# Negated gates at the end of a later pool, DRAM weight sums in 2 KB packets at other places, and the loaded sum first in its tile

## The chip, the cores and the metric

The kernel runs on one core of a Trainium2 chip. The metric is the device time of one execution in microseconds (us); the profile is of one execution, whose span begins with its first instruction. Engines are named as in the profile: PE (matrix unit; PEld is its weight load), DVE, ACT, POOL, and SP, which here only issues DMAs. The granted clock is the share of PE's full clock that the throttle let through.

## The reference, cut to what matters

Two layers over 512 latent tokens and 256 context tokens, width 1024, all float32. Layer 0 mixes tokens by windowed attention with a sink, layer 1 by retention in both directions; after each stands a SwiGLU feed-forward network (FFN). Both are modulated by a shift, scale and gate (adaLN).

```python
def modulate(h, shift, scale):
    return h * (1 + scale) + shift

def swiglu(h, w_in, w_out):
    gate, up = jnp.split(h @ w_in, 2, axis=-1)
    return (jax.nn.silu(gate) * up) @ w_out
```

The kernel needs float32 accuracy from a matrix unit that is given operands in a shorter form. Each float32 tile is therefore split into a high part (a cast on ACT) and a low part (the difference, on DVE), and each product is three matmuls: high by high, low by high, high by low.

## The kernel before, in words

**Order.** The code is written in the order of the data. A planner then orders the instructions of each engine by estimates of when operands are ready and results due; `after(ins, others)` (L97) adds an order that the planner has to keep, with no wait of its own. Each engine runs its own list strictly in order. A tile name with a number of buffers rotates through them: a new tile waits until the old content has been read.

**Attention (about 100 to 322 us).** `attend` (L800) does one block of queries for one group of four heads; the loop at L909 makes 24 such turns, 0 to 23, six for each of four groups. Between them `make_q` (L583) makes the queries of two heads: after turns 1, 3, 7, 9 and 13 for the pairs j = 3 to 7, and once ahead of the loop for j = 2. For j from 2 to 6 the high half is cast into a tile `y0` with one buffer, the low half into `hn`, and four DMAs for each token stream bring the halves to their partitions (L626, issued by SP). Tiles `k1`, `k2` of the keys come from `key_parts` (L568). At turns late in the loop the residual streams are loaded (L180, L187) and the weights of the output projection Wo (L128), both on SP.

**The FFN of layer 0 (about 421 to 776 us).** The FFN is written as a seven-product scheme on 2 x 2 blocks, so it needs sums of weight blocks. For positions 2 to 21 two of the sums are made ahead in DRAM: `gu_sum`, five positions in each of four batches, and for the output weights `fo_sum` in two batches. `sum_copy` (L828) copies a weight block to DRAM on SP's queue; `sum_add` (L831) adds another with a DMA that accumulates, on POOL's queue. Each batch of `gu_sum` takes two copies and two adds (1280 KB each), each batch of `fo_sum` four copies and four adds, of which two copies start from the sum made before. `spread` hangs these steps on turns: a step is issued behind the last copy of that turn's block. Turns from 100 on are positions of the FFN. Each step on SP or POOL that depends on an earlier one waits there, and what is behind it in that queue waits too.

`seven(pos)` (L1123) does one position: it loads two weight tiles `g` and `u` and the sum `t1` (L1127 to L1130), splits g into b11, t1 into w1 (`bhi`, `blo`), forms two more weight sums on DVE (L1136, L1137), splits them into b24 (`whi`, `wlo`), splits u into b3, and runs seven products at L970: in the order that PE gets, Y from b11, X from b11, Z from w1, Y from b24 and so on. The c11 add (L1150) brings Y and X together on DVE ahead of the first silu. In most positions one step of the next layer's adaLN vectors (L276, L279) is done as well.

**Output products (776 to about 985 us).** `fo_product` (L1197) runs pairs of positions; for each it loads the tokens (`fo_tokens`) and weights (`fo_weights`, L1185), splits them and multiplies at L1207. Its argument `ahead` says behind which pair's first product other work may go. `fo_add` (L1212) adds the result to the residual stream, with a gate or, where the scheme subtracts, with the negated gate `ngate`.

**Pools.** SBUF is shared out by pools that lie one behind the other: those of one side from the bottom, those of the other side (`side="right"`) from the top. `cp`, in which `ngate` lies (64 bytes in each partition), is the first on the left; the pools opened after it on that side, `ap`, `ep`, `fp` and so on, stand above it. `T(pool, cols, name, bufs)` takes a tile from a pool.

Of the kernel before, what the change touches and what calls it, by code (L numbers as in the profile page):

```python
# [8 lines left out]
F32 = mybir.dt.float32  # L9
# [5 lines left out]
P = 128  # L15
# [8 lines left out]
FT = DFF // P  # L24
FFN_GROUPS = (2, 4, 4, 4, 4, 4)
PAIRS = FT // 2
TURN = [p + PAIRS * j for p in range(PAIRS) for j in range(2)]
GU_BATCH, GU_BATCHES = 5, 4
ROW = 8192
FO_BATCHES = (6, 5)  # L30
RH = 4
EPS = 1e-6
# [22 lines left out]
def dit_kernel(ctx, tc, xT, cT, crow, small, consts, masks, tabs0, tabs1, jtab, adaQ, adaN, adaT, wst, wgu, wfo, out):  # L55
    nc = tc.nc
    mult, add, sub = ALU.mult, ALU.add, ALU.subtract
# [9 lines left out]
    def T(pool, cols, tag, bufs, dt=F32):  # L67
        return pool.tile([P, cols], dt, tag=tag, bufs=bufs, name=tag)

    def pj(n=512):  # L70
# [10 lines left out]
    mods = {(l, s): cp.tile([P, 6, 8], F32, name=f"mod{l}{s}") for l in range(2) for s in range(2)}  # L81
    acol = {(l, s, w): cp.tile([P, 8], F32, name=f"acol{l}{s}{w}")
            for l, s, w in ((0, 0, 0), (0, 1, 0), (0, 0, 1), (0, 1, 1), (1, 0, 0), (1, 1, 0), (1, 0, 1))}
    ngate = cp.tile([P, 2, 8], F32, name="ngate")
    gm2 = cp.tile([P, 32], F32, name="gm2")
    nc.vector.tensor_scalar(gm2, sm_t[:, C_G:C_G + 32], -2.0, None, op0=mult)
    qk_gain = cp.tile([P, 2], F32, name="qk_gain")
# [9 lines left out]
    def after(ins, others):  # L97
        for o in others:
            tc.add_manual_dep(ins.ins, o.ins.name, order, reason="table set turn")
# [69 lines left out]
    def split(t, hi, lo, behind=()):  # L169
        after(nc.scalar.copy(hi, t), behind)  # L170
        return nc.vector.tensor_tensor(lo, t, hi, op=sub)  # L171
# [389 lines left out]
    At = ExitStack()  # L561
    ap = At.enter_context(tc.tile_pool(name="ap", bufs=1, reuse_waits="tile"))

    kx, kc = {}, {}
    off_grid(ap, 16)

    def key_parts(e, src, tag="k", bufs=8):
        if tag == "kc":  # L568
            both = T(akv, 1024, tag, bufs, F32R)
            k1, k2 = both[:, 0:512], both[:, 512:1024]  # L570
        else:
            k1, k2 = T(akv, 512, tag, bufs, F32R), T(akv, 512, tag, bufs, F32R)
        src = src[64 * e:64 * e + 64, :]
        nc.scalar.copy(k1[0:64, :], src)
        nc.scalar.copy(k2[64:128, :], src)
        hi_same = (k1[0:64, :], k2[64:128, :])[e]
        nc.vector.tensor_tensor(k1[64:128, :], src, hi_same, op=sub)
        nc.vector.tensor_tensor(k2[0:64, :], src, hi_same, op=sub)
        return k1, k2

    q, stats, norm_end = {}, {}, []
# [81 lines left out]
    with tc.manual_schedule(engines={mybir.EngineType.PE}):  # L663
        q0[0]()
        key_factor(1)
        for e in range(2):
            kx[e] = key_parts(e, kn[0])
        q0[1]()
        c1()
        for e in range(2):  # L670
            k1, k2 = key_parts(e, kn[1], "kc", 2)
            kc[e], kc[2 + e] = ((k1[:, c], k2[:, c]) for c in HALVES)
        q0[2]()
        values(0, 3)
        q0[3]()
        values(1, 2)
        values(1, 3)
# [147 lines left out]
    fo_sum = [dp.tile([4, n, P, 512], F32, name=f"fo_sum{b}") for b, n in enumerate(FO_BATCHES)]  # L825

    def sum_copy(dst, src, behind):
        after(nc.sync.dma_start(flat(dst), flat(src)), [behind])  # L828

    def sum_add(dst, src, behind):  # L830
        after(nc.gpsimd.dma_start(flat(dst), flat(src), accum_op=add, max_dma_last_dim=ROW), [behind])  # L831
# [1 line left out]
    def gu_steps(b):  # L833
        rows = slice(2 + b * GU_BATCH, 2 + (b + 1) * GU_BATCH)
        t = gu_sum[b]
        return [lambda a: sum_copy(t[0], wgu[0, rows], a), lambda a: sum_copy(t[1], wgu[2, rows], a),
                lambda a: sum_add(t[0], wgu[2, rows], a), lambda a: sum_add(t[1], wgu[3, rows], a)]

    def fo_steps(b):
        rows = slice(sum(FO_BATCHES[:b]), sum(FO_BATCHES[:b + 1]))  # L840
        t = fo_sum[b]
        return [lambda a: sum_copy(t[3], wfo[0, rows], a), lambda a: sum_copy(t[2], wfo[2, rows], a),
                lambda a: sum_add(t[3], wfo[2, rows], a), lambda a: sum_add(t[2], wfo[3, rows], a),
                lambda a: sum_copy(t[0], t[3], a), lambda a: sum_add(t[0], wfo[3, rows], a),
                lambda a: sum_copy(t[1], t[0], a), lambda a: sum_add(t[1], wfo[1, rows], a)]

    sum_turns = {}

    def spread(steps, turns):
        for st, n in zip(steps, turns):  # L850
            sum_turns.setdefault(n, []).append(st)

    spread(gu_steps(0), (1, 2, 4, 5))
    spread(gu_steps(1), (5, 6, 8, 9))
    spread(gu_steps(2), (9, 10, 12, 13))
    spread(gu_steps(3), (13, 14, 16, 17))
    spread(fo_steps(0), (3, 7, 11, 15, 17, 19, 21, 23))
    spread(fo_steps(1), range(102, 118, 2))

    for piece in make_q(1):  # L860
        piece()
    rope_key(kn[2])
# [30 lines left out]
    early = [2, 3, 0, 1]  # L893
# [224 lines left out]
    def ada_next(behind):  # L1118

        if ada_q:  # L1120
            ada_tile(*ada_q.pop(0), cr, [behind], fp)

    def seven(pos):  # L1123
        g, u = raw_turn(), raw_turn()
        t1 = op_t()[:, 0:512]
        sums = gu_sum[(pos - 2) // GU_BATCH][:, (pos - 2) % GU_BATCH]
        nc.sync.dma_start(two(g), rows_of(wgu[0:2, pos]))  # L1127
        nc.sync.dma_start(t1, sums[0])
        nc.sync.dma_start(u[:, 512:1024], wgu[3, pos])
        nc.sync.dma_start(u[:, 0:512], sums[1])  # L1130
        l_, r_ = slice(0, 512), slice(512, 1024)
        b11 = w_parts(fp, 1)
        split(g, *b11)
        w1 = T(fp, 512, "bhi", 1, F32R), T(fp, 512, "blo", 1, F32R)
        split(t1, *w1)
        nc.vector.tensor_tensor(g[:, l_], t1, u[:, r_], op=add)  # L1136
        nc.vector.tensor_tensor(g[:, r_], g[:, r_], g[:, l_], op=add)  # L1137
        b24 = w_parts(fp, 1)
        half = split(g, *b24)
        b3 = w_parts(fp, 1)  # L1140
        split(u, *b3)
        if cr:
            ada_next(half)
        X, Y, Z = bank("X"), bank("Y"), bank("Z")
        c11, c12, c22, c21 = t_hn(384), t_hn(384), t_sq(384), t_sq(384)
        a = new_act(pos % 2)
        product(Y, operand["11"], b11, 0, True)
        nc.scalar.copy(c11, Y)
        product(X, operand["12"], b11, 512, True)
        nc.vector.tensor_tensor(c11, c11, X, op=add)  # L1150
        silu(c11, c11)
        product(Y, operand[2], b24, 0, False)
        nc.scalar.copy(c12, Y)
        product(Z, operand[1], w1, 0, True)
        nc.scalar.copy(c21, Z)
        product(Y, operand[3], b3, 0, False)
        nc.scalar.copy(c22, Y)
        nc.vector.tensor_tensor(c22, c21, c22, op=sub)
        product(Z, operand[4], b3, 512, False)
        nc.vector.tensor_tensor(c12, Z, c12, op=sub)  # L1160
        finish_half(a, 0, c11, c12)
        product(Y, operand["22"], b24, 512, False)
        silu(c21, Y)
        end = finish_half(a, 1, c21, c22)
        return pair_sums() if pos % 2 else end
# [24 lines left out]
    def fo_tokens(i, m, n):  # L1190
        raw = op_t()
        load = nc.sync.dma_start(raw[:, 0:384 * n].rearrange("p (a n) -> p a n", a=n), rows_of(saved[m][i, 0:n]))
        x = T(ep, WIDE, "aq", 8, F32R), T(ep, WIDE, "aq", 8, F32R)
        split(raw[:, 0:384 * n], *(t[:, 0:384 * n] for t in x))
        return x, load

    def fo_product(o, i, kind, first, per_step=(), ahead={}):  # L1197
        for m in range((PAIRS + 1) // 2):
            n = min(2, PAIRS - 2 * m)
            x, load = fo_tokens(i, m, n)  # L1200
            w = fo_weights(kind, m, n, load)
            for j in range(n):
                xs = [t[:, j * 384:(j + 1) * 384] for t in x]
                for d in range(4):
                    ws = slice(j * 512 + d * P, j * 512 + (d + 1) * P)
                    for e, (p, r) in enumerate(((w[0], xs[0]), (w[1], xs[0]), (w[0], xs[1]))):
                        ins = nc.tensor.matmul(o[d], p[:, ws], r, start=first and 2 * m + j + e == 0,  # L1207
                                               stop=2 * m + j == PAIRS - 1 and e == 2, skip_group_check=True)
                        if j + d + e == 0 and m in ahead:
                            late, n_late = ahead[m]  # L1210
                            after(ins, late[:n_late])
            for go in per_step[m:m + 1]:  # L1212
                go(ins)
# [56 lines left out]
    for pos in range(2, FT):  # L1270
        if pos == 2:
            last_sum()
        end = seven(pos)
        if pos == 2:
            ends.pop(0)()
            for s in range(2):
                nc.vector.tensor_scalar(ngate[:, s], mods[0, s][:, 5], -1.0, None, op0=mult)
        if pos == 4:
            cr = cond_rows(fp)
        for st in sum_turns.get(100 + pos, ()):  # L1280
            st(end)
        if pos > 3 and pos % 6 != 5:
            ada_next(end)
# [60 lines left out]

    early, ctx_sum = [], []
    y = [bank("Y"), bank("Y"), bank("Z"), bank("Z")]
    fo_product(y, 3, 5, True, [first_half, first_half_norm], {3: (early, 1), 4: (early, 2)})
    fo_add(y, 0, 1)
    F.close()
    E.close()  # L1350
# [775 lines left out]
```

## Time and profile before

| | |
|---|---|
| median of 3 runs (range) | 1815.34 us (1812.19 to 1816.35) |
| profiled execution | 1814.74 us |
| its span | 1813.0 us |
| mean granted clock of PE | 0.985 |
| PE busy | 1730.4 us (95%) |
| DVE, ACT, POOL busy | 1336.5, 890.4, 112.3 us |
| DMA | 98216 packets, 297.83 MB, mean 164 GB/s |

The page gives busy time of each engine over the span, the granted clock and the DMA share by slices, the queues, the chain of work that ended last, and the costliest groups of instructions. The views of the trace that the prediction uses are: waits (an engine and line, what it waited for, total us, times, longest), stretches (busy time of each engine between two times, with clock and DMA share), DMA issues (line of the program, size, median time to landing) and instructions in order of time (start, length, engine, line, out<-in).

### The profile page before, as it was taken

What the parts mean: (1) busy time and instruction counts of PE and PEld (TensorE: products, weight loads), DVE (VectorE), ACT (ScalarE), POOL (GpSimd) and SP (SyncE); (2) the same over time, 40 slices, a digit from 0 to 9 for tenths busy, and PEclk for the clock granted to TensorE, in tenths of its full rate; (3) what the DMA queues carried; (4) which work ended last, traced back from release to release, by engine and by line L of the source; (5) the groups of instructions that cost most, each with busy time, mean ns of one, the idle gap of its engine ahead of it and who ended that gap; (6) DMA issues with size and microseconds to landing.
All of it is one profiled execution on the core that took longest, in us unless ns stands there. A gap on an engine that the chain in (4) does not pass through costs nothing.

```text
span 1813.0 us, 27982 instructions
## 1 busy us (share of the span) xinstructions
PE 1730.4 (95%) x10798; PEld 1548.3 (85%) x10798; DVE 1336.5 (74%) x2385; ACT 890.4 (49%) x1555; POOL 112.3 (6%) x246
## 2 busy tenths in 40 slices
PE   8999989998888988989998999999999999999999
PEld 5877767898888888889997889889888899999998
DVE  6787668796676676777778876776757898777874
ACT  5586668464333333344455453534534564445442
POOL 0001111000111111110000000000000010000000
PEclk9999899999999999999999999999999999999999
DMA  9538788644476657589735471453533333333332
GB/s 374 191 106 233 204 210 227 221 140 166 154 214 212 198 186 209 180 317 306 264 115 143 106 208 48 129 163 77 169 105 95 103 106 104 94 116 96 104 92 82
DMA packets 98216, 297.83 MB, mean 164 GB/s; under 512 B 10161, under 2 KB 22209, under 8 KB 94625
## 3 DMA queue, kind: packets, MB, share of 16 engines
q1 hardware_dynamic: 80656, 222.69, 36.8%
q0 software_dynamic: 17136, 72.82, 16.5%
q8 instruction: 85, 1.39, 0.3%
q10 hardware_dynamic: 288, 0.52, 0.1%
q14 instruction: 51, 0.41, 0.1%
HBM read 274.82 MB, written 61.28 MB: 185 GB/s over the span
## 4 chain that ended last, share of the span: by engine, by line
PE 48%; DVE 3%; DMA 3%; issue 1%; ACT 1%; DVEq 0%; ACTq 0%
PE Z L1443 7%; PE Y L970 6%; PE Y L1432 3%; PE Z L970 3%; PE pj L1443 2%; PE pj L153 2%; PE pj L155 2%; PE pj L154 2%; PE X L1432 2%; PE X L970 1%; DMA adaw<-in_adaT_dram 1%; PE X L1443 1%; PE Y L1207 1%; PE Z L1207 1%; PE Y L154 1%
## 5 line engine op out<-in xcount | busy, mean ns | idle before, releaser
L171 DVE TENSOR_TENSOR wlo<-wraw,whi 128x1024 fp32r<-128x1024 f32 (+1 forms) x285 | 343.5, 1209 | 95.7 <-ACT whi L170 94.9
L170 ACT CAST whi<-wraw 128x1024 fp32r<-128x1024 f32 (+1 forms) x285 | 293.8, 1038 | 234.6 <-DMA wraw<-in_wst_dram 46.2
L970 PE MATMUL Y<-aq,whi 128*128 128x384 f32 x640 | 181.1, 346 | 2.1 <-ACT whi L170 2.1
L970 PEld LDWEIGHTS Y<-aq,whi 128*128 128x128 f32 x640 | 119.7, 192 | 8.6 <-ACT whi L170 4.3
L970 PE MATMUL Y<-aq,wlo 128*128 128x384 f32 x320 | 109.5, 342 | 2.8 <-DVE wlo L171 2.8
L279 DVE CUSTOM_DVE_ANT_0 y<-adaw,crow,small_sb 128x1024 bf16<-128x1024 f32 x64 | 82.0, 1282 | 39.2 <-DMA adaw<-in_adaT_dram 38.8
L1443 PE MATMUL Z<-whi,sA 128*128 128x512 f32 x256 | 81.3, 394 | 0.0
L107 ACT ACTIVATE pr<-pr,stat,qs 128x513 f32<-128x513 f32 (+2 forms) x96 | 74.2, 774 | 9.6 <-DVE stat L735 8.1
L170 ACT CAST aq<-op 128x768 fp32r<-128x768 f32 (+1 forms) x62 | 41.8, 692 | 57.6 <-PE pj L1207 27.8
L155 PE MATMUL pj<-ax,whi 128*128 128x512 f32 x176 | 68.9, 392 | 0.0
L153 PE MATMUL pj<-ax,whi 128*128 128x512 f32 x176 | 68.8, 391 | 0.0
L154 PE MATMUL pj<-ax,wlo 128*128 128x512 f32 x176 | 68.8, 391 | 0.0
L970 PEld LDWEIGHTS Y<-aq,wlo 128*128 128x128 f32 x320 | 61.4, 192 | 4.7 <-DVE wlo L171 4.4
L754 PE MATMUL pT<-const_sb,pr 128*128 128x128 f32 x352 | 56.2, 283 | 9.6 <-ACT pr L743 4.8
L970 PE MATMUL Z<-aq,bhi 128*128 128x384 f32 x160 | 49.5, 373 | 13.6 <-ACT bhi L170 13.6
L970 PE MATMUL Y<-sA,whi 128*128 128x256 f32 x304 | 59.8, 281 | 0.0
L262 DVE SCALAR_TENSOR_TENSOR res<-pj,mod,res 128x512 f32<-128x512 f32 (+1 forms) x64 | 45.4, 714 | 18.9 <-PE pj L155 18.7
L729 DVE CUSTOM_DVE_ANT_0 pr<-S,mask,qs 128x256 f32<-128x256 f32 (+1 forms) x96 | 53.4, 569 | 7.2 <-PE S L728 5.3
L970 PE MATMUL Y<-hx,whi 128*128 128x256 f32 x304 | 57.8, 281 | 0.0
L754 PEld LDWEIGHTS pT<-const_sb,pr 128*128 128x128 f32 x352 | 40.9, 143 | 19.5 <-ACT pr L743 5.5
L1443 PEld LDWEIGHTS Z<-whi,sA 128*128 128x128 f32 x256 | 48.2, 188 | 10.8
L1207 PE MATMUL Y<-aq,whi 128*128 128x384 f32 x176 | 53.2, 342 | 3.7 <-ACT whi L170 3.7
(595 smaller groups left out, 5153.9 us busy)
## 6 DMA issues: line engine op xcount, KB each, us to landing
wraw<-in_wst_dram SPq DMA_DIRECT2D x158, 512.0 KB, 3.7
adaw<-in_adaT_dram POOLq DMA_DIRECT2D x48, 512.0 KB, 4.4
op<-saved SPq DMA_DIRECT2D x35, 384.0 KB, 6.2
saved<-op POOLq DMA_DIRECT2D x33, 384.0 KB, 2.9
wraw<-in_wgu_dram SPq DMA_DIRECT2D x24, 512.0 KB, 3.9
gu_sum<-in_wgu_dram SPq DMA_DIRECT2D x8, 1280.0 KB, 7.8
gu_sum<-in_wgu_dram POOLq DMA_DIRECT2D x8, 1280.0 KB, 14.2
wraw<-fo_sum SPq DMA_DIRECT2D x20, 512.0 KB, 4.8
```

What stands on the lines that cost most here:

```text
L107: ins = nc.scalar.activation(*args, **kw)
L153: nc.tensor.matmul(o, whi, xhi, start=first, stop=False)
L154: nc.tensor.matmul(o, wlo, xhi, start=False, stop=False)
L155: return nc.tensor.matmul(o, whi, xlo, start=False, stop=last)
L170: after(nc.scalar.copy(hi, t), behind)
L171: return nc.vector.tensor_tensor(lo, t, hi, op=sub)
L279: res.append(nc.vector.tensor_tensor_reduce(junk, w, cr[:, s * 1024:(s + 1) * 1024], 1.0, sm_t[:, C_ADAB + l * 48 + j:C_ADAB + l * 48 + j ...
L754: nc.tensor.transpose(tp[:, a * P:(a + 1) * P], self.pr[(0, 2, 1, 3)[a]][:, ki * P:(ki + 1) * P], ident)
L970: nc.tensor.matmul(o, p, r, start=first and k + i == 0, stop=k == 3 and i == 2, skip_group_check=not first)
L1207: ins = nc.tensor.matmul(o[d], p[:, ws], r, start=first and 2 * m + j + e == 0, stop=2 * m + j == PAIRS - 1 and e == 2, skip_group_check=True)
L1432: ins = nc.tensor.matmul(o[:, e * SC:(e + 1) * SC], p[:, ws], r, start=first and k + e + i == 0, stop=k == 3 and i == 2, skip_group_check= ...
L1443: ins = nc.tensor.matmul(os[t], p, r, start=first and k + i == 0, stop=k == 3 and i == 2, skip_group_check=by_k or not first)
```

## The change

- The DRAM sums move in packets of at most 2048 bytes, the copies too, which had no limit; the adds had 8192.
- The steps stand at other turns. The four copies of the first two batches are hung on a new place, -1, right behind the first key parts and ahead of attention.
- `ngate` is taken from pool `fp` at position 2, when all that stays in that pool is there, and not from `cp`.
- In `seven`, `t1` is loaded first and g behind it; the c11 add is ordered behind the low half of w1.
- The loads and splits of the first output product's first pair are issued inside the last position (`fo_ahead`).
- In the last `fo_product`, work that stood behind pair 4 stands behind pair 5.

```diff
-ROW = 8192
+ROW = 2048
...
-    ngate = cp.tile([P, 2, 8], F32, name="ngate")
...
-        nc.vector.tensor_tensor(k2[0:64, :], src, hi_same, op=sub)
+        key_end[:] = [nc.vector.tensor_tensor(k2[0:64, :], src, hi_same, op=sub)]
...
             kx[e] = key_parts(e, kn[0])
+        keys_end = key_end[0]
...
-        after(nc.sync.dma_start(flat(dst), flat(src)), [behind])
+        after(nc.sync.dma_start(flat(dst), flat(src), max_dma_last_dim=ROW), [behind])
...
-    spread(gu_steps(0), (1, 2, 4, 5))
-    spread(gu_steps(1), (5, 6, 8, 9))
-    spread(gu_steps(2), (9, 10, 12, 13))
-    spread(gu_steps(3), (13, 14, 16, 17))
-    spread(fo_steps(0), (3, 7, 11, 15, 17, 19, 21, 23))
-    spread(fo_steps(1), range(102, 118, 2))
-
+    spread(gu_steps(0), (-1, -1, 1, 1))
+    spread(gu_steps(1), (-1, -1, 4, 4))
+    spread(gu_steps(2), (7, 7, 10, 10))
+    spread(gu_steps(3), (14, 14, 16, 16))
+    spread(fo_steps(0), (8, 8, 14, 14, 16, 18, 20, 22))
+    spread(fo_steps(1), (19, 19, 21, 21, 23, 103, 105, 107))
+
+    for st in sum_turns[-1]:
+        st(keys_end)
...
-        nc.sync.dma_start(two(g), rows_of(wgu[0:2, pos]))
-        nc.sync.dma_start(t1, sums[0])
+        first = nc.sync.dma_start(t1, sums[0])
+        after(nc.sync.dma_start(two(g), rows_of(wgu[0:2, pos])), [first])
...
-        split(t1, *w1)
+        w1_low = split(t1, *w1)
...
+        if pos == FT - 1:
+            fo_ahead.append(fo_step(0, 0, 0))
...
-        nc.vector.tensor_tensor(c11, c11, X, op=add)
+        after(nc.vector.tensor_tensor(c11, c11, X, op=add), [w1_low])
...
+    def fo_step(i, kind, m):
+        n = min(2, PAIRS - 2 * m)
+        x, load = fo_tokens(i, m, n)
+        return x, fo_weights(kind, m, n, load)
+
+    fo_ahead = []
+
...
-            x, load = fo_tokens(i, m, n)
-            w = fo_weights(kind, m, n, load)
+            x, w = fo_ahead.pop() if fo_ahead else fo_step(i, kind, m)
...
             ends.pop(0)()
+            ngate = T(fp, 16, "ngate", 1).rearrange("p (s d) -> p s d", s=2)
...
-    fo_product(y, 3, 5, True, [first_half, first_half_norm], {3: (early, 1), 4: (early, 2)})
+    fo_product(y, 3, 5, True, [first_half, first_half_norm], {3: (early, 1), 5: (early, 2)})
```

2 lines of the change are left out of this document (1 added, 1 removed).

## The prediction

> **What bounds the kernel now.** I read the page's busy row and clock row first, then the stretches (busy time of each engine by stage), and in the stages where TensorE is not full the waits and the order of instructions.
>
> ```profile
> PE 1730.4 (95%) x10798; PEld 1548.3 (85%) x10798; DVE 1336.5 (74%) x2385; ACT 890.4 (49%) x1555; POOL 112.3 (6%) x246
> ...
> q1 hardware_dynamic: 80656, 222.69, 36.8%
> q0 software_dynamic: 17136, 72.82, 16.5%
> ```
>
> ```profile
> 100.00:120.00 20.00, 18.57 (x123) 14.82 (x122) 19.29 (x61) 17.12 (x35) 1.90 (x11) 1.00 0.10 24
> 160.00:180.00 20.00, 17.42 (x137) 14.32 (x135) 13.96 (x43) 12.44 (x25) 2.14 (x8) 1.00 0.99 258
> 180.00:200.00 20.00, 19.42 (x131) 15.97 (x131) 13.70 (x35) 15.24 (x31) 2.84 (x10) 0.91 0.65 166
> 200.00:220.00 20.00, 15.98 (x96) 13.70 (x92) 11.96 (x53) 10.54 (x31) 1.43 (x8) 0.83 0.91 252
> 240.00:260.00 20.00, 15.17 (x82) 11.70 (x81) 10.01 (x35) 10.13 (x23) 0.77 (x5) 0.83 0.78 226
> 280.00:300.00 20.00, 19.98 (x162) 15.46 (x161) 18.23 (x66) 16.32 (x44) 4.11 (x12) 1.00 1.02 238
> ...
> 421.00:776.00 355.00, 317.41 (x1706) 300.34 (x1695) 243.75 (x371) 130.11 (x207) 47.23 (x74) 0.97 0.62 197
> 776.00:800.00 24.00, 18.73 (x94) 18.23 (x95) 18.55 (x24) 12.25 (x15) 3.85 (x8) 0.86 0.84 295
> 940.00:1000.00 60.00, 54.90 (x297) 48.64 (x296) 47.78 (x101) 34.55 (x67) 2.73 (x4) 0.95 0.44 124
> 1000.00:1500.00 500.00, 498.23 (x2791) 432.60 (x2790) 369.59 (x547) 237.99 (x367) 20.34 (x27) 1.00 0.43 120
> 1500.00:1790.00 290.00, 289.97 (x2042) 271.24 (x2041) 220.74 (x306) 136.25 (x227) 0.00 (x0) 1.00 0.32 99
> ```
>
> The first fence holds busy time, share and count of each engine, and two DMA queues (packets, MB, share of 16 engines' time). In the second each row is a stretch in us from the start: its length, busy time (and count) of PE, PEld, DVE, ACT and POOL, then the granted clock of TensorE, the DMA share and GB/s.
>
> TensorE bounds it, so time can come from two places: stretches in which PE idles, and what one matmul costs. From 1000 us on PE is full and the granted clock 1.00: only the cost of a matmul counts there. Before that I price a stretch as length less PE busy, plus (1 − clock) × length, since at a lower clock the same work takes that much longer. Attention, the four rows from 160 to 260: idle 2.58 + 0.58 + 4.02 + 4.83 = 12.0, clock 1.8 + 3.4 + 3.4 = 8.6, together 20.6 us. First feed-forward stage (421 to 776, twenty positions): 37.6 + 10.6 = 48 us. Start of its output products (776 to 800): 5.3 + 3.4 = 8.6. The stretch 940 to 1000: 5.1 + 3.0 = 8.1. These are the ceilings of what can be won there.
>
> **Attention: packets and places of the sums.** The waits of 100 to 325 us, and the DMA issues of 190 to 265 us (KB each, median us to landing):
>
> ```profile
> ACT y L170 <- DMA q<-y: 14.3, 3, 5.5
> PE pT L754 <- ACT pr L743: 4.8, 1, 4.8
> PE pT L754 <- DVE stat L735: 4.0, 1, 4.0
> ```
>
> ```profile
> gu_sum<-in_wgu_dram POOLq DMA_DIRECT2D x4, 1280.0 KB, 12.2
> gu_sum<-in_wgu_dram SPq DMA_DIRECT2D x3, 1280.0 KB, 7.2
> q<-y SPq DMA_DIRECT2D x4, 128.0 KB, 10.1
> q<-y SPq DMA_DIRECT2D x4, 64.0 KB, 1.9
> ```
>
> The 4.0 and 4.8 us PE waits are named after DVE and ACT, but both engines stand behind ACT's cast of y, which has a single buffer and may not write it before the previous q transfer has read it: three waits, 14.3 us. Those transfers are small, yet take 10.1 us with sums in flight and 1.9 us (at half the size) without. The longest wait is 5.5 us, so a q transfer some 5.5 us shorter removes all three. The change does two things to them. It cuts the sums' packets to 2 KB: by the two queue rows a packet on the software queue now takes 16.5% × 16 × 1813 / 17136 = 279 ns at a mean of 4.2 KB, one on the hardware queue 132 ns at 2.8 KB. A q packet that shares an engine with a sum then waits for a quarter as many bytes each time; estimate 2 + (10.1 − 2)/4 = 4 us at best, 10.1 at worst (bytes, not packets, set it). I take 5, nearer the hardware queue's row. And it moves the sums: the four first copies go right behind the first key parts, ahead of the 100 to 120 row with its DMA share of 0.10, where four copies of 7.2 us have room; without that cover they would push the adds at turns 1 and 4 back. Adds then fall on turns 1, 4, 10 and 16, against q transfers after turns 1, 3, 7, 9, 13: the one at turn 10 still meets the last q group. Gain: 0 to 20.6; I take **11**, two of three stalls with their clock windows.
>
> The row says transfers stretch with what else is in flight. The Trainium skill, "DMA: Bandwidth & Descriptors", section "Queues, rings and completion order", says that each DMA engine goes round the queues packet by packet; by that the shorter packets alone would remove the stalls (20 us). Its "Rules for kernel authors" asks for bigger transfers; by that the sums only get longer and the gain is nearer 0. No row here tells them apart.
>
> **The price: later DMA traffic.** Seven steps more than now land between turns 14 and 23, about 250 to 320 us, while the 280 to 300 row already has a DMA share of 1.02. SP and POOL issue in order: a copy waiting for an add holds the later loads of res and of the output projection's weights behind it. PE idles 0.02 us in that row, so nothing there is late yet. The cost is between 0 and one add's whole landing (12.2 us); I take **+4**, nearer the end that the idle time speaks for.
>
> **First feed-forward stage: the loaded sum first.** The waits of 421 to 776 us, and one position (start, duration, engine, line):
>
> ```profile
> PE Z L970 <- DVE blo L171: 18.5, 16, 2.9
> PE Z L970 <- ACT bhi L170: 13.6, 8, 1.8
> ```
>
> ```profile
> 567.61 1.28 DVE L279 CUSTOM_DVE_ANT_0 y<-adaw,crow,small_sb 128x1024 bf16<-128x1024 f32 x1
> 568.08 0.33 PE L970 MATMUL Z<-aq,bhi 128*128 128x384 f32 x1
> 568.82 0.55 DVE L1150 TENSOR_TENSOR hn<-hn,X 128x384 f32<-128x384 f32 x1
> 569.28 0.68 DVE L1136 TENSOR_TENSOR wraw<-op,wraw 128x512 f32<-128x512 f32 x1
> 569.88 0.69 DVE L171 TENSOR_TENSOR blo<-op,bhi 128x512 fp32r<-128x512 f32 x1
> 570.49 0.69 DVE L1137 TENSOR_TENSOR wraw<-wraw 128x512 f32<-128x512 f32 x1
> 570.62 0.44 PE L970 MATMUL Z<-aq,blo 128*128 128x384 f32 x1 [2.21 <-DVE blo L171]
> 571.21 2.00 ACT L170 CAST whi<-wraw 128x1024 fp32r<-128x1024 f32 x2 [1.28 <-DVE wraw L1137]
> 573.65 0.52 PE L970 MATMUL Y<-aq,whi 128*128 128x384 f32 x1
> ```
>
> Product Z needs bhi and blo of the loaded sum. In this position blo stands on DVE behind the add to c11 (L1150) and L1136, and PE waits 2.21 us; in the eight of the second row the cast to bhi itself is late on ACT. 32.1 us of waits in all, and the clock windows that follow them (10.6). The change loads the sum before g, and orders the add behind blo. Then blo can start right behind the scalar-shift step (L279), at 568.8 or, ahead of it, at 567.6, and Z is held up by 1 us at most. But the next product (b24) needs L1136, L1137 and whi. Z's twelve matmuls from 568.08 on take 12 × 317.41 / 1706 = 2.2 us unheld, to 570.3. With blo first and the add, L1136 and L1137 behind it, DVE's four end about when they do now, L1137 at 571.2, and whi's first half is cast a microsecond later: Y would start near 572.2, not 573.65. So of what a position loses 1.5 us come back, and 2 us remain as a new wait; where L1136 and L1137, which need only loads, are put ahead of the add, most of that goes too. Gain between 48 (all idle and clock) and −10 (twenty positions each 0.5 worse); I take **25**, half of the ceiling and near 20 × 1.5 less the positions in which the wait was shorter. Behind the add stand the silu and c12's copy on ACT; they move back by blo's 0.7 us, and PE needs them only products later. Also SP now issues g after t1: g loses part of its lead, and the b11 split behind it; a position lasts 355 / 20 = 17.7 us and the largest transfer of the DMA fence above 12.2, so I cost it at nothing; were the lead gone, the b11 wait would come in on top, and that is the −10.
>
> **Output products, and the copies ahead.** Waits of 774 to 800 us, then of 955 to 1000 us:
>
> ```profile
> ACT whi L170 <- DMA wraw<-in_wfo_dram: 4.8, 1, 4.8
> ```
>
> ```profile
> PEld pj L1243 <- ACT sq L1242: 2.5, 1, 2.5
> ```
>
> The first product's loads go into the last position: the cast's DMA wait of 4.8 goes, and with it most of the stretch's 5.3 us of PE idle. 0 to 8.6, I take **5**. One more product ahead of L1243: 0 to 2.5 plus a clock window of 1.7, I take **2**.
>
> **Negated gates in another pool.** It holds 64 bytes per partition; without it every pool on its side of SBUF after it starts 64 bytes lower. Does an address cost anything? Two stretches of the second feed-forward stage with the same 24 matmuls (line, shape, names), only other buffers:
>
> ```profile
> 1635.27 0.28 PE L970 MATMUL Z<-sA,whi 128*128 128x256 f32 x1
> ...
> 1638.01 0.28 PE L970 MATMUL X<-hx,whi 128*128 128x256 f32 x1
> ```
>
> ```profile
> 1645.09 0.28 PE L970 MATMUL Z<-sA,whi 128*128 128x256 f32 x1
> ...
> 1647.96 0.28 PE L970 MATMUL X<-hx,whi 128*128 128x256 f32 x1
> ```
>
> 2.74 / 24 = 114 ns against 2.87 / 24 = 120 ns, both at full clock. In the compiled program the weights of the first lie 64 bytes off a multiple of 256, those of the second on one; the moving tile on one both times. Where hx moves (192 off) with weights on a multiple, starts lie as close as in the fast pair; with weights 64 off, as far apart as in the slow one. After the shift nearly all of this stage has weights on a multiple and the moving tile 192 off, the 114 class. The 1500 to 1790 row counts 2042 matmuls: 2042 × 5.4 ns = 11 us if all were slow now; about half are, 5.5 us. The wider products of the projections fall into such classes too; I add half again. Bounds: 15 to −6 (a class that I misread). I take **8**.
>
> This is a reading of intervals and not a mechanism I know. The Trainium skill, "SBUF — State Buffer", section "SBUF: two separate sides", says that PE's access never waits on anyone; by that the move is worth 0 and the sum 8 us higher. The 114 against 120 speaks for a cost by place.
>
> **Sum.** 1814.74 (profiled run: span 1813.0 and 1.7 around it; 0.6 under the median 1815.34) − 11 + 4 − 25 − 5 − 2 − 8 = **1768 us**.
>
> **Rivals.**
> - *The wait moves to b24* (or the planner keeps bhi behind the silu): FFN gives 5, not 25: 1788. For it: DVE's chain above, DVE busy 244 of 355. Against: L1136 and L1137 need only loads and can go earlier.
> - *The FFN stalls go altogether*, no clock windows left: 45, so 1748. For it: L1136 waits for loads alone. Against: the same chain.
> - *Addresses do nothing*: 1776. For it the page; against it the row pairs.
> - *Slower: SP's queue blocks at turns 16 to 23.* Three copies wait there for an add each, and if traffic doubles an add to 24 us SP stands 73 us; with half of it covered by the loads' lead the output projection's weights come 37 us late, and with the b24 wait taking all of the FFN's gain the rest is −26: 1826. It ends slower once SP's hold costs PE more than 26. For it the share of 1.02; against it that PE idles nowhere in that row.
> - *Nothing moves*: attention stalls stay, FFN swaps wait for wait, within 0.2%: about 1813.
>
> **Numbers.** Chances: forecast 0.42, b24 0.22, all stalls gone 0.12, addresses 0.12, slower 0.07, nothing 0.05. Range 1742 to 1803: from the third rival less its spread to the second's with attention at 0. Own range of the forecast: 1755 to 1782. A change under 0.2% (3.6 us) can't be told from none: faster 0.88, same 0.05, slower 0.07.
>
> **What would show it.** Right: no ACT wait for q over 2 us and clock 1.00 from 180 to 260; Z's waits for blo and bhi under 10 us in sum, and positions near 16.5 us; no 4.8 us wait at 776; the second feed-forward stage shorter with the same matmuls; 300 to 380 us as before. Wrong: a Y wait on whi or wlo of 1 us or more in each position; new PE idle after 322 us behind a weight load; L970 intervals unchanged.

## The result, and the profile after

The changed kernel takes 1866.59 us (median of 4 runs, 1863.27 to 1868.75), the kernel before, in the same measurement, 1813.99 us (1812.19 to 1816.35): a ratio of 1.0288, 95% interval 1.0264 to 1.0311. It is **2.9% slower**. The forecast was 1768, its range 1742 to 1803.

Where the time went is seen by cutting both profiled executions (spans 1813.0 and 1867.0) at the same matmuls: first and last score of attention, first product of the first feed-forward stage, first output product, first product of retention at L1432 (L1443 after), first and last product of the second feed-forward stage. The stretches of the kernel before (columns as in the prediction):

```profile
95.20:316.00 220.80, 205.44 (x1453) 166.36 (x1453) 170.33 (x562) 162.00 (x373) 28.18 (x106) 0.96 0.74 198
316.00:421.60 105.60, 105.33 (x692) 92.36 (x691) 86.63 (x158) 59.89 (x115) 2.09 (x3) 1.00 0.52 168
421.60:779.60 358.00, 316.81 (x1683) 299.94 (x1682) 246.12 (x375) 133.08 (x210) 48.60 (x77) 0.97 0.61 196
779.60:982.10 202.50, 194.03 (x1041) 186.38 (x1042) 149.97 (x238) 98.25 (x148) 12.07 (x22) 0.97 0.74 242
982.10:1506.60 524.50, 519.69 (x2932) 452.46 (x2931) 394.06 (x591) 251.26 (x389) 20.34 (x27) 1.00 0.42 115
1506.60:1786.50 279.90, 279.87 (x1999) 263.31 (x1998) 212.67 (x293) 130.24 (x219) 0.00 (x0) 1.00 0.33 102
```

The same stretches of the changed kernel:

```profile
93.60:296.50 202.90, 197.34 (x1435) 158.71 (x1435) 168.97 (x559) 159.25 (x370) 29.05 (x106) 1.00 0.78 186
296.50:424.40 127.90, 111.09 (x711) 96.15 (x709) 90.93 (x173) 63.36 (x123) 5.61 (x7) 0.93 0.65 195
424.40:843.20 418.80, 340.17 (x1680) 322.33 (x1681) 244.50 (x359) 130.48 (x202) 44.35 (x70) 0.90 0.46 152
843.20:1048.00 204.80, 192.87 (x1042) 184.64 (x1041) 150.79 (x241) 100.04 (x150) 13.68 (x25) 0.98 0.73 239
1048.00:1566.00 518.00, 512.07 (x2932) 447.72 (x2931) 392.75 (x590) 251.63 (x389) 20.36 (x27) 1.00 0.42 117
1566.00:1840.10 274.10, 274.07 (x1998) 257.42 (x1997) 212.71 (x293) 130.22 (x219) 0.00 (x0) 1.00 0.35 103
```

Attention −17.9, output projection +22.3, **first feed-forward stage +60.8**, output products +2.3, retention −6.5, second feed-forward stage −5.8; the start −1.6 and the tail +0.4 make up the 54.0 of the spans. One stage outweighs all the gains. There PE idles 418.80 − 340.17 = 78.6 us, before 41.2, which is 37.4 more; and the same products keep PE busy 23.4 us longer (340.17 against 316.81), with the granted clock at 0.90 against 0.97. The two make up the 60.8.

The waits of PE in that stage, after (424 to 845 us); before they were 18.5 and 13.6:

```profile
PE Z L972 <- DVE blo L170: 51.2, 20, 5.0
PE Z L972 <- ACT bhi L169: 25.5, 20, 4.8
```

So Z waits in each of the 20 positions, for the very tile that is now loaded first. The start of one position after, PE, ACT and DVE (start, length):

```profile
614.73 0.34 PE L972 MATMUL Y<-aq,whi 128*128 128x384 f32 x1
615.11 0.49 ACT L112 ACTIVATE sq<-Y 128x384 f32<-128x384 f32 x1 [3.63 <-PE Y L972]
615.49 0.61 ACT L169 CAST bhi<-op 128x512 fp32r<-128x512 f32 x1
615.63 0.56 DVE L1058 TENSOR_TENSOR op<-sq 128x384 f32<-128x384 f32 x1 [1.46 <-ACT sq L112]
616.00 1.99 ACT L169 CAST whi<-wraw 128x1024 fp32r<-128x1024 f32 x2
616.10 1.28 DVE L278 CUSTOM_DVE_ANT_0 y<-adaw,crow,small_sb 128x1024 bf16<-128x1024 f32 x1
616.16 0.45 PE L972 MATMUL Z<-aq,bhi 128*128 128x384 f32 x1 [1.09 <-ACT bhi L169]
617.31 0.69 DVE L170 TENSOR_TENSOR blo<-op,bhi 128x512 fp32r<-128x512 f32 x1
618.05 0.44 PE L972 MATMUL Z<-aq,blo 128*128 128x384 f32 x1 [1.45 <-DVE blo L170]
```

The last product of the position before (Y, 614.73) feeds the last silu (ACT, 615.11). Only behind that silu come the cast of bhi and the cast of b11 (one of the two at 616.00, the other is b3's), and on DVE the product of the halves (L1058) and a scalar-shift step come ahead of blo. Z from w1, the first product of the new position, has nothing to run ahead of it. Before, b11 was split 7 to 11 us ahead of that silu: its cast is the second of the two casts that the prediction shows at 571.21, for the position that begins near 583. Its low half follows on DVE at 576.24, PE reads it at 583.07, and the silu comes at 583.27. So PE had Y and X from b11 to run while bhi and blo were made (kernel before, DVE, PE, ACT):

```profile
576.24 1.22 DVE L171 TENSOR_TENSOR wlo<-wraw,whi 128x1024 fp32r<-128x1024 f32 x1
...
583.07 0.33 PE L970 MATMUL Y<-aq,wlo 128*128 128x384 f32 x1
...
583.27 0.49 ACT L113 ACTIVATE sq<-Y 128x384 f32<-128x384 f32 x1 [1.04 <-PE Y L970]
```

The other loss is at the change to the output projection. Waits of the changed kernel, of PE near 320 us and of SP's queue from 265 to 345 us, and SP's issues around them:

```profile
PE pj L152 <- ACT h L169: 7.1, 1, 7.1
PE pj L152 <- DVE res L261: 4.1, 1, 4.1
ACT whi L169 <- DMA wraw<-in_wst_dram: 10.3, 4, 8.4
```

```profile
SPq L828 <- DMA fo_sum<-in_wfo_dram: 24.0, 2, 23.3
...
271.19 1.17 SPq L828 DMA_DIRECT2D fo_sum<-in_wfo_dram  x2
295.77 0.48 SPq L828 DMA_DIRECT2D fo_sum<-fo_sum  x1
296.35 1.55 SPq L179 DMA_DIRECT2D res<-in_xT_dram  x3
297.99 3.03 SPq L127 DMA_DIRECT2D wraw<-in_wst_dram  x2
```

SP stands 23.3 us, from 272 to 295.8, behind a copy of one sum to the next that waits for an add. That add was issued at 262.60 and took 33.2 us to land; in the kernel before, the median of the four adds of this size was 13.1. Residual and weight loads follow only then, and PE's 7.1 us wait at 313 ends with a cast of h that stands on ACT behind a weight cast which waited 8.4 us for its load. Not all of the 22.3 us is of this kind: at the end of the stretch PE waits 4.8 us for bhi, ahead of the first product of the FFN, and that belongs to the load order (t1_only below has it with the sums as before).

What went well is attention: ACT no longer waits for q at all. The DMA issues of 160 to 262 us, after:

```profile
gu_sum<-in_wgu_dram SPq DMA_DIRECT2D x4, 1280.0 KB, 13.6
gu_sum<-in_wgu_dram POOLq DMA_DIRECT2D x4, 1280.0 KB, 17.1
q<-y SPq DMA_DIRECT2D x6, 128.0 KB, 3.0
```

The q transfers take 3.0 us, not 10.1; the price is on the sums themselves, 13.6 and 17.1 us in the place of 7.2 and 12.2.

### The profile page after: what moved, and what is told of

The parts are those of the page before. It is cut to its first block, busy times and chain, and to the rows that moved or that the text cites. A ratio compares the mean times of both kernels' runs of the same rounds, so it can differ in the third digit from the quotient of the medians.

```text
span 1867.0 us, 27979 instructions
## 1 busy us (share of the span) xinstructions
PE 1736.2 (93%) x10798; PEld 1554.5 (83%) x10798; DVE 1337.3 (72%) x2385; ACT 890.7 (48%) x1555; POOL 114.1 (6%) x246
## 3 DMA queue, kind: packets, MB, share of 16 engines
q0 software_dynamic: 25200, 72.82, 16.3%
## 4 chain that ended last, share of the span: by engine, by line
PE 57%; DVE 6%; DMA 3%; issue 3%; ACT 2%; POOL 0%; DVEq 0%; POOLq 0%; ACTq 0%; SPq 0%
PE Y L972 12%; PE Z L1454 6%; PE Z L972 6%; PE Y L1443 3%; PE X L972 3%; DMA adaw<-in_adaT_dram 2%; PE pj L152 2%; PE pj L154 2%; PE pj L153 2%; PE pj L1454 2%; PE Y L1217 2%; PE Z L1217 2%; PE X L1217 1%; PE pj L1217 1%; PE X L1443 1%
## 5 line engine op out<-in xcount | busy, mean ns | idle before, releaser
L972 PE MATMUL Y<-aq,whi 128*128 128x384 f32 x640 | 189.3, 358 | 6.2 <-ACT hn L1157 5.6
L972 PEld LDWEIGHTS Y<-aq,whi 128*128 128x128 f32 x640 | 128.1, 205 | 10.0 <-ACT hn L1157 9.0
L972 PE MATMUL Y<-aq,wlo 128*128 128x384 f32 x320 | 114.5, 358 | 0.0
L972 PE MATMUL Z<-aq,blo 128*128 128x384 f32 x80 | 36.3, 454 | 51.2 <-DVE blo L170 51.2
L972 PE MATMUL Z<-aq,bhi 128*128 128x384 f32 x160 | 56.3, 417 | 25.5 <-ACT bhi L169 25.5
L1162 DVE TENSOR_TENSOR sq<-sq 128x384 f32<-128x384 f32 x20 | 11.2, 560 | 80.3 <-ACT sq L1161 80.3
L972 PEld LDWEIGHTS Y<-aq,wlo 128*128 128x128 f32 x320 | 65.9, 206 | 2.2 <-DVE wlo L170 2.2
L972 PEld LDWEIGHTS Z<-aq,blo 128*128 128x128 f32 x80 | 19.7, 246 | 56.5 <-DVE blo L170 56.5
L972 PEld LDWEIGHTS Z<-aq,bhi 128*128 128x128 f32 x160 | 36.8, 235 | 31.7 <-ACT bhi L169 31.7
L152 PE MATMUL pj<-h,whi 128*128 128x512 f32 x120 | 49.8, 415 | 11.2 <-ACT h L169 7.1
```

Source lines behind the costliest of these rows:

```text
L152: nc.tensor.matmul(o, whi, xhi, start=first, stop=False)
L972: nc.tensor.matmul(o, p, r, start=first and k + i == 0, stop=k == 3 and i == 2, skip_group_check=not first)
```

## The experiments

All times below are medians, with the kernel before measured on the same chip in the same job. The table gives each kernel's stages, cut at the same matmuls as above (us in the one profiled execution, so a difference of a few us can be chance). In fo_only, after_no_t1 and best the first output product starts about 9 us ahead of the end of the last position, so there the first FFN looks shorter and the output products longer.

| kernel | attention | to the FFN | first FFN | output products | retention | second FFN |
|---|---|---|---|---|---|---|
| before | 220.8 | 105.6 | 358.0 | 202.5 | 524.5 | 279.9 |
| after | 202.9 | 127.9 | 418.8 | 204.8 | 518.0 | 274.1 |
| t1_only | 219.5 | 111.4 | 414.8 | 199.9 | 525.3 | 279.6 |
| t1_pinned | 218.8 | 113.5 | 436.8 | 198.5 | 525.0 | 279.8 |
| t1_lead | 219.5 | 111.1 | 351.2 | 200.9 | 523.9 | 279.5 |
| add_only | 218.3 | 105.6 | 343.4 | 199.9 | 524.7 | 279.7 |
| ngate_only | 221.0 | 104.1 | 359.1 | 198.8 | 518.4 | 273.3 |
| ngate_pad | 221.4 | 105.3 | 358.2 | 199.6 | 525.2 | 279.8 |
| sums_only | 204.3 | 123.2 | 357.2 | 199.4 | 524.1 | 279.6 |
| sums_mix | 210.1 | 105.3 | 358.3 | 201.3 | 523.0 | 279.7 |
| row_only | 213.1 | 105.6 | 358.8 | 200.9 | 524.0 | 279.7 |
| fo_only | 222.7 | 105.6 | 345.9 | 214.3 | 525.4 | 279.8 |
| after_no_t1 | 203.6 | 121.8 | 339.2 | 212.5 | 521.2 | 275.0 |
| best | 211.4 | 104.0 | 328.9 | 213.6 | 519.1 | 274.1 |

**t1_only: the forced order of the two loads alone.** The c11 add is as before.

```diff
-        nc.sync.dma_start(two(g), rows_of(wgu[0:2, pos]))
-        nc.sync.dma_start(t1, sums[0])
+        first = nc.sync.dma_start(t1, sums[0])
+        after(nc.sync.dma_start(two(g), rows_of(wgu[0:2, pos])), [first])
```

> The kernel before with one edit: t1 is loaded first and g behind it. Theory: this edit alone turns the planner's order of the products round, so that Z from w1 leads the position in place of Y and X from b11, and then waits for bhi and blo, which stand behind the tail of the position before: feed-forward stage 358 to about 415 us, whole kernel 1865 to 1880. Rival: the stage is slow because of 2 KB packets or because steps of the sums fall into it; then this kernel stays within 10 us of 1814.

1876.32 against 1812.2, ratio 1.0355 (1.0335 to 1.0375). The first FFN takes 414.8 us, nearly all of the loss of the changed kernel, and 111.4 us pass to the FFN, 5.8 more than before. This one edit is the cause; packets and sums are not (sums_only below has 357.2 us in this stage). One position of this kernel, SP's loads and ACT's casts for it:

```profile
613.31 0.38 SPq L1127 DMA_DIRECT2D op<-gu_sum  x1
613.73 0.43 SPq L1128 DMA_DIRECT2D wraw<-in_wgu_dram  x1
```

```profile
626.10 0.49 ACT L113 ACTIVATE sq<-Y 128x384 f32<-128x384 f32 x1 [1.02 <-PE Y L970]
626.48 0.61 ACT L170 CAST bhi<-op 128x512 fp32r<-128x512 f32 x1
626.99 1.05 ACT L170 CAST whi<-wraw 128x1024 fp32r<-128x1024 f32 x1
```

t1 and g are issued 13 us before bhi and b11 are cast, and the cast waits for the silu in front of it, not for a DMA. One position earlier they were issued 30 us ahead (575.82 and 576.40), and the casts stand behind the silu all the same (606.88, the silu at 606.49). In the whole stage ACT waits 2.7 us for the position's loads. So the loads are not late; the engines' order of work is.

**t1_pinned: t1 first, order of the products as before.**

```diff
-        product(X, operand["12"], b11, 512, True)
+        x_end = product(X, operand["12"], b11, 512, True)
...
-        product(Z, operand[1], w1, 0, True)
+        product(Z, operand[1], w1, 0, True, [x_end])
```

(The first matmul of this Z is ordered behind `x_end`; the load order is that of t1_only.)

> As t1_only, but the first matmul of Z from w1 is ordered behind the last of X from b11, as in the kernel before. Theory (order of products): the feed-forward stage comes back to 358 us or less, whole kernel 1790 to 1818. Rival (g, issued behind t1, has lost its lead and b11 is late): stays above 1850, with PE waits on whi or wlo at the head of a position.

1897.59, ratio 1.0469 (1.0448 to 1.049): worse than t1_only. So the first theory, that the order of the products is the loss, fell. Its PE waits (421 to 860 us) are no longer for w1 but for b11:

```profile
PE Y L970 <- DVE wlo L171: 48.8, 20, 5.0
PE Y L970 <- ACT whi L170: 45.9, 20, 7.3
```

With Y and X from b11 in front again, these wait for b11's split, which still stands behind the last silu and after bhi (silu at 617.73, bhi at 618.12, the casts of b11 and b3 at 618.62). The time and the waits are those that the rival named; its cause, a late load of g, is not borne out, since ACT waits 2.5 us in all for these loads in the stage. What is left is the place of the split in the lists of ACT and DVE.

**t1_lead: loads as in t1_only, the split of b11 ahead of the last silu.** `lead(pos)` holds the loads of `seven` (t1 first, g behind it) and the split of b11, and returns the low half last.

```diff
         product(Y, operand["22"], b24, 512, False)
+        if pos < FT - 1:
+            led.append(lead(pos + 1))
         silu(c21, Y)
+        for d in led:
+            after(turn["silu"][-1], [d[4]])
```

> As t1_only (t1 loaded first, g behind it), but the loads of the next position and the split of its b11 are written ahead of the last silu of a position, and that silu is ordered behind the low half of b11. Theory (the loads land in time; what costs is that b11's split, and all that follows, stands behind that silu on ACT and DVE): the feed-forward stage loses at least half of the 60 us, whole kernel 1790 to 1840. Rival (g's load itself comes late once it stands behind t1): stays above 1860, with ACT waiting for a DMA at the cast of b11.

1809.61, ratio 0.9988 (0.9968 to 1.0008): the loss is gone, with t1 still loaded ahead of g. The first FFN takes 351.2 us. Z's waits are 37.4 us, for 76.1 in t1_only and 32.1 before. The loads are not earlier for it: in one position t1 and g are issued at 603.88 and 604.40 and bhi is cast at 611.90, 8 us later. This shows that the loss is the place of the split behind the last silu, and not the load order as such. Why the planner moves the split when g is tied to t1 can't be seen in a trace. What the trace shows is what the tie takes away: before, SP issued g 23 us ahead of the t1 of the same position (570.04 and 592.97). That the planner then expects t1's buffer or the loads late is my reading, and was not tried.

**add_only: the c11 add behind blo.**

```diff
-        split(t1, *w1)
+        w1_low = split(t1, *w1)
...
-        nc.vector.tensor_tensor(c11, c11, X, op=add)
+        after(nc.vector.tensor_tensor(c11, c11, X, op=add), [w1_low])
```

> The kernel before with one edit: the c11 add is ordered behind blo. Theory: order of the products stays, Z's 18.5 us of waits for blo go down by half or more, whole kernel 1790 to 1808. Rival (the wait moves to b24, whose sums now stand behind): within 5 us of 1814, with new waits of Y on whi or wlo in the place of those for blo.

1794.55, ratio 0.9901 (0.9884 to 0.9919). The gain is there, but not as either side put it. The PE waits of its stage:

```profile
PE Z L970 <- DVE blo L171: 17.5, 17, 2.2
PE Y L970 <- DVE wlo L171: 8.9, 16, 0.6
...
PE Z L970 <- ACT bhi L170: 1.2, 1, 1.2
```

Waits for blo hardly fall (18.5 to 17.5); those for bhi do (13.6 to 1.2), since the silu that stood ahead of the cast now comes later with the add. A wait of Y on wlo grows from 2.8 to 8.9, in pieces of 0.6 at most. In the stretch of the stage PE idles 32.8 us, for 41.2 before, and the clock is 0.99, against 0.97; of the 14.6 us, 8.4 are less idle time and 6.2 shorter busy time of PE:

```profile
419.40:762.80 343.40, 310.59 (x1684) 293.10 (x1683) 245.11 (x375) 131.92 (x210) 48.80 (x77) 0.99 0.64 204
```

**ngate_only, ngate_pad: 64 bytes.** In the first, `ngate` is taken from `fp`; the second adds 64 unused bytes to `cp`, so that all pools are back where they were.

```diff
-    ngate = cp.tile([P, 2, 8], F32, name="ngate")
...
+            ngate = T(fp, 16, "ngate", 1).rearrange("p (s d) -> p s d", s=2)
...
(ngate_pad, besides)
+    nc.gpsimd.memset(cp.tile([P, 16], F32, name="pad"), 0.0)
```

> The kernel before with one edit: ngate in pool fp, so that all pools above cp lie 64 bytes lower. Theory (the interval of matmuls depends on where their operands lie): second feed-forward stage and retention 5 to 7 us shorter each, as in the changed kernel, whole kernel 1799 to 1807. Rival (places cost nothing; what was won there came from another edit): within 3 us of 1814.

> As ngate_only, but 64 unused bytes are taken from pool cp, so that every pool lies where it lay in the kernel before. Theory (places of the operands): the gain is gone, 1809 to 1815. Rival (it is the move of ngate itself, or the order of instructions that comes with it): 1797 to 1801 as in ngate_only.

1798.36, ratio 0.992 (0.9901 to 0.9939), just below the range expected; then with the pad 1814.82, ratio 1.001 (0.9995 to 1.0026). The gain comes with the places and goes with them. Retention and the second FFN, ngate_only, then ngate_pad:

```profile
977.00:1495.40 518.40, 513.28 (x2932) 448.08 (x2931) 392.68 (x590) 251.56 (x389) 20.42 (x27) 1.00 0.42 117
1495.40:1768.70 273.30, 273.27 (x1999) 257.15 (x1998) 212.54 (x293) 130.28 (x219) 0.00 (x0) 1.00 0.34 104
```

```profile
979.30:1504.50 525.20, 520.61 (x2932) 452.03 (x2931) 393.55 (x590) 251.46 (x389) 20.34 (x27) 1.00 0.41 115
1504.50:1784.30 279.80, 279.80 (x1998) 263.29 (x1997) 212.81 (x293) 130.11 (x219) 0.00 (x0) 1.00 0.34 102
```

The same number of matmuls, PE full, clock 1.00 in all four rows: 273.3 against 279.8 us. The same 24 matmuls as in the prediction's two stretches, in the changed kernel:

```profile
1762.54 0.28 PE L972 MATMUL Z<-sA,whi 128*128 128x256 f32 x1
...
1765.26 0.28 PE L972 MATMUL X<-hx,whi 128*128 128x256 f32 x1
```

2.72 / 24 = 113 ns: the faster class.

**sums_only, sums_mix, row_only: the sums in DRAM.** sums_only has the packets and all the new turns, sums_mix leaves the steps of `fo_sum` at their old turns, row_only has the 2 KB packets and no other edit.

```diff
(sums_only and sums_mix)
+    spread(gu_steps(0), (-1, -1, 1, 1))
+    spread(gu_steps(1), (-1, -1, 4, 4))
+    spread(gu_steps(2), (7, 7, 10, 10))
+    spread(gu_steps(3), (14, 14, 16, 16))
(sums_only)
+    spread(fo_steps(0), (8, 8, 14, 14, 16, 18, 20, 22))
+    spread(fo_steps(1), (19, 19, 21, 21, 23, 103, 105, 107))
(sums_mix)
+    spread(fo_steps(0), (3, 7, 11, 15, 17, 19, 21, 23))
+    spread(fo_steps(1), range(102, 118, 2))
```

> The kernel before with 2 KB packets, copies too, and all steps of the sums at their new turns, nothing else. Theory, from the stages of the changed kernel: attention 16 us shorter, output projection 20 us longer, whole kernel 1810 to 1820, with the 7 and 4 us waits of PE behind residual and weight loads near 320 us. Rival (those two waits come from the other edits): 1793 to 1800.

> As sums_only, but the steps of the two fo_sum batches stay at the turns of the kernel before; the gu_sum steps move. Theory (SP held behind copies of fo_sum that wait for adds at turns 16 to 23 makes the output projection late): attention keeps its 16 us, the waits near 320 us go, 1792 to 1802. Rival (2 KB packets or gu_sum's adds at turn 16 make it late): 1808 to 1818.

> The kernel before with 2 KB packets for adds and copies, the steps at their old turns. Theory (shorter packets shorten the q transfers): the three ACT waits for q fall from 14.3 us to under 4, attention 10 to 16 us shorter, whole kernel 1798 to 1805. Rival (only the places of the sums matter): ACT waits for q above 8 us, 1810 to 1816.

sums_only: 1812.74, ratio 1.0 (0.9985 to 1.0014). Attention 16.5 us shorter and the output projection 17.6 longer, with the same waits of PE, the longer of them 6.6 us.

sums_mix: 1808.03, ratio 0.9972 (0.9955 to 0.9988). They are gone and the projection is back at 105.3, so it is the steps of `fo_sum` that held SP. Attention keeps 10.7 of the 16.5. The median lies in the rival's range, above the 1792 to 1802 of the theory: three of the ten executions took 1801 to 1803 us, the other seven 1807 to 1812. The profiled one (1801.71) is of the three, so the 10.7 stands for them; what sets the two groups apart stays open. row_only: 1807.63, ratio 0.9976 (0.9957 to 0.9995), attention 7.7 us shorter; what ACT waits for q:

```profile
ACT y L170 <- DMA q<-y: 8.1, 3, 3.0
```

The time lies between the two expectations; the 8.1 us is not below the 4 of the theory and just above the 8 of the rival. So shorter packets do about half of the work in attention (7.7 of 16.5 us), the places the rest. The DMA issues of 190 to 265 us show an add at 13.5 us and a copy at 7.2 here, for 12.2 and 7.2 before: most of the longer landings of the changed kernel (17.1 and 13.6) come with the places and not with the packets.

**fo_only: the first output product in the last position**, and pair 5 for pair 4 (the edits as in the diff of the change).

> The kernel before with the first output product's pair issued in the last position, and pair 5 in the place of pair 4, nothing else. Theory of the prediction: the 4.8 us DMA wait at 776 us goes, whole kernel 1804 to 1809. Rival (its splits stand behind the last position's work on ACT and DVE anyway, so PE waits as long): 1811 to 1816.

1814.09, ratio 1.0 (0.9983 to 1.0017): nothing in time, as the rival had it. In the table 12 us move from the first FFN to the output products, as the first of these now starts earlier; then Y waits:

```profile
PE Y L1215 <- DVE wlo L171: 8.3, 3, 3.7
```

The DMA wait that was to go is still there, 4.6 us ahead of a weight cast on ACT at 790.66. In the kernel before it ended at 788.46, at the fourth weight cast of the output products, whose load SP issued at 782.57; the first pair's load had been issued at 751.96, even ahead of the last position. So the edit moved a load that was not waited for. Pair 5 did its part: PE's wait for ACT at L1243 went from 2.1 to 0.6 us, too little to show in the time.

**after_no_t1, best: the change with parts undone.** after_no_t1 is the changed kernel with the two loads as before; best also leaves the steps of `fo_sum` at their old turns.

```diff
-        first = nc.sync.dma_start(t1, sums[0])
-        after(nc.sync.dma_start(two(g), rows_of(wgu[0:2, pos])), [first])
+        nc.sync.dma_start(two(g), rows_of(wgu[0:2, pos]))
+        nc.sync.dma_start(t1, sums[0])
(best, besides)
-    spread(fo_steps(0), (8, 8, 14, 14, 16, 18, 20, 22))
-    spread(fo_steps(1), (19, 19, 21, 21, 23, 103, 105, 107))
+    spread(fo_steps(0), (3, 7, 11, 15, 17, 19, 21, 23))
+    spread(fo_steps(1), range(102, 118, 2))
```

> The changed kernel with one part undone: g is loaded first again and t1 is free; the rest, with the c11 add behind blo, stays. Theory (the forced order of the two loads is the whole loss): 1813 less 14 for ngate, 18 for the add, 0 for the sums, 0 to 6 for the first output product, so 1774 to 1783. Rival (other parts lose in the feed-forward stage too, once together): above 1790.

> As after_no_t1, with the steps of the two fo_sum batches back at the turns of the kernel before. Theory (gains add up): 5 us below after_no_t1, 1769 to 1778. Rival (what the sums win in attention is lost elsewhere when the rest is faster): the same as after_no_t1.

after_no_t1: 1792.64, ratio 0.9893 (0.9854 to 0.9932), 10 us above what was expected: the forced load order is not the whole loss, and the rival holds. best: 1772.87, ratio **0.9776** (0.9743 to 0.9808): it beats both kernels. It lies in the range expected, but by luck, since that range was to come from 5 us below after_no_t1 and it is 20 below. The difference lies in the output projection (121.8 against 104.0) and the first FFN (339.2 against 328.9), less what attention gives back (203.6 against 211.4). In the first FFN after_no_t1 shows the `fo_sum` steps in a second place, POOL's queue; POOL and DVE:

```profile
526.96 1.24 POOL L831 DMA_DIRECT2D fo_sum<-in_wfo_dram  x1
527.69 1.09 POOL L275 DMA_DIRECT2D adaw<-in_adaT_dram  x1
```

```profile
543.37 1.28 DVE L278 CUSTOM_DVE_ANT_0 y<-adaw,crow,small_sb 128x1024 bf16<-128x1024 f32 x1 [10.78 <-DMA adaw<-in_adaT_dram]
```

The add of turn 107 is issued just ahead of a load of adaLN weights, which then comes 16 us after its issue; DVE waits 10.78 us for it with the tail of a position behind it. In best the longest such wait of the stage is 4.9 us, though in sum these waits hardly differ (17.3 and 16.5 us). PE waits 26.1 us for bhi and blo in this stage, in best 17.9; that this comes from the one long wait is argued and not tested.

## Why the prediction was wrong

- **First feed-forward stage, forecast −25, measured +60.8.** The step that failed is "so I cost it at nothing; were the lead gone, the b11 wait would come in on top, and that is the −10". I took the new load order for a matter of landing times alone, in a list of instructions that otherwise stays. The loads did land in time (ACT waits 2.7 us for them in the stage in t1_only). But the planner made a new list: the split of b11 went behind the last silu of the position before, beside that of w1, so that a position begins with nothing to multiply. t1_only shows the loss, t1_lead that it goes when the split gets its place back. Z, which was to be held up by 1 us at most, waits 76.7 us in the 20 positions, 3.8 in each. So the bound of −10, twenty times 0.5, was far too small: PE idles 37.4 us more and, at a clock of 0.90 for 0.97, is busy 23.4 us longer. The first rival allowed for a planner that keeps bhi behind a silu, but as a smaller gain and not as a loss.
- **The c11 add behind blo** was right in sign: add_only won 17.7 us (1812.2 − 1794.55). The way was another: bhi's waits went and blo's stayed, and the new wait on b24 stayed at 0.6 us at most, not 2. The two casts at 571.21 are also not halves of b24, as I read them, but b24's and the next position's b11.
- **Attention, forecast −11 of at most 20.6, measured −17.9.** The mechanism held (q transfers 3.0 us, ACT's wait gone). It was under-sized: I left one of three stalls standing, and none stood. The Trainium skill, "DMA: Bandwidth & Descriptors", section "Queues, rings and completion order", says that each DMA engine goes round the queues packet by packet. By that, I held, the packets alone would have done it; row_only gains 7.7 us and has 8.1 us of waits left, so the trace agrees in part. The argument from bigger transfers had nothing to act on, since a sum's transfer stayed at 1280 KB.
- **Later DMA traffic, forecast +4 with 12.2 as bound, measured +17.6** in sums_only, of the +22.3 in this stage; 5.8 of it comes with the load order alone (t1_only). The place was named rightly, SP behind a copy that waits for an add, but the size was not: I bounded it by one add's landing of 12.2 us, and this add took 33.2, of which SP stood 23.3. My argument that PE idled nowhere there before said nothing of how late the loads behind it would become. The rival "slower" named this queue too; the change did end slower, but by the feed-forward stage, so that its sign came true is luck.
- **Start of the output products, −5, and pair 5, −2.** fo_only measured nothing. I took the 4.8 us DMA wait for one on the first pair's load; before, it stood at the fourth weight cast, and the first pair's load was out ahead of the last position already; the wait is still 4.6 us. Of the wait behind pair 4, 1.5 us went.
- **Places of the operands, forecast −8, measured −6.5 and −5.8 in the two late stages**, and −13.8 in all in ngate_only (1798.36 − 1812.2), within the bounds, at their far end. The second FFN's own term, 5.5, came out at 5.8 and 6.6; the half that was added for the wider products was too small, as retention alone gave 6.1 to 6.5.
- **The range** left out 1866 since each term's loss was bounded by landing times; none allowed for a new order. Its upper end, 1803, is also 4 us more than the 1788 and 11 that it is said to come from.

## What to carry to other kernels

An order forced between two loads is, under a planner, an edit to every engine's list: before costing it by landing times, ask which work hangs on the load that is moved back, and look where that work would stand if it were taken up only at the end of what came before. A transfer that waits in an in-order queue is paid for by all that is behind it: see what follows it in that queue, SP or POOL. And where PE is full at clock 1.00, compare the same matmuls on different buffers: moving 64 bytes was worth 0.8% here.

## What the runs showed of the hardware

The interval of a matmul depends on where its operands lie: the same 24 matmuls take 2.87 or 2.72 us, and 64 bytes taken from a pool and given back move the whole kernel by 0.9% (ratios 0.992 and 1.001 to the kernel before). The prediction sorted the places by their remainder to 256 bytes and foretold the 114 ns class; 113 came. But the runs tried one shift of 64 bytes, so no run shows that 256 is the period. The Trainium skill, "SBUF — State Buffer", section "SBUF: two separate sides", says that PE never waits on anyone there. It speaks of engines that share a port and does not foretell this cost; the measurement decides. What in the port or the array causes it was not tried.

The software queue's row of the changed kernel's page:

```profile
q0 software_dynamic: 25200, 72.82, 16.3%
```

It carries the same 72.82 MB as before in 25200 packets, for 17136. The shares are of different spans: 16.3% of 1867.0 us is 304 us for each engine, and 16.5% of 1813.0 is 299. So smaller packets cost about 2% more engine time on this queue here; row_only, with the packets alone, has 17.0% of 1803.8 us, 307.
